# The 60 taps of a convolution, spread over the stages ahead of the attention's second pair

## The chip, the cores and the metric

The kernel runs on one core of a Trainium2 chip. Its engines each follow an instruction queue of their own: TensorE (PE in the profile; its weight loads are PEld), VectorE (DVE), ScalarE (ACT), GpSimd (POOL) and SyncE (SP, which here only issues DMAs). The metric is the time of one execution on the device in microseconds (us).

## What is computed

One layer of a hybrid decoder trunk, 1024 positions of 1024 features, all in float32: an input projection feeds three groups of heads, whose outputs go through one output projection; a gated MLP with a short causal convolution follows.

```
h = rmsnorm(x, ln1_g)
p = h @ w_in
qa, ka, va, log_f        # 6 heads: forgetting attention
qb, kb, vb               # 6 heads: dilated sliding windows
yc = p[..., GV] * sigmoid(p[..., GG])          # 256 channels
yc = causal_dwconv(yc, conv_w, conv_b)         # 31 taps per channel
yc = silu(layernorm(yc, cnorm_g, cnorm_b))
y = concatenate([rmsnorm(ya), rmsnorm(yb), yc])
x = x + y @ w_o
u = causal_dwconv(rmsnorm(x, ln2_g) @ w_up, ffn_conv_w, ffn_conv_b)   # 3 taps
x = x + (silu(u[..., :F]) * u[..., F:]) @ w_down
out = rmsnorm(x, g_final)
```

## The kernel before

Features lie on the partitions and the 1024 positions along a row, so a tile is 128 x 1024, mostly worked on as two halves of 512. Every float32 operand of a matmul is split into a high and a low part (names with `h` and `l`), and a product takes three matmuls (`mm3`, lines 118 to 120). ScalarE copies the high part, GpSimd or VectorE subtracts it to get the low one. Weights come by DMA on SP's queue into two raw buffers (`raw_...`) and are split into `wh_...` (ScalarE) and `wl_...` (GpSimd, line 105), three buffers each.

The part around the change runs in this order. The first gates (`gv0`, `gg0`) are projected while x is loaded. ScalarE takes the sigmoid of `gg` and VectorE multiplies (`gate_mul`, line 259): the product of channel group 0 is `gv` again, `us[0]`. Eight blocks of v (`vps`, lines 278 to 280) follow, each of 24 matmuls into one of two PSUM buffers of tag `mm`. ScalarE copies each out to `vf` (two buffers, line 282) and casts it to three tiles `VS` (line 285); GpSimd adds the forget gates' bias (`fg`, line 287) and takes the low parts (line 286). A block's `vf` is free when GpSimd is done with it. Then come the second gates (`g`, line 254 evicts them), the small logarithm of the forget gates on VectorE (`lf_...`, lines 489 to 501), the first q and k (`qps`, `kps`; VectorE evicts them at lines 298 and 314, ScalarE and GpSimd split them into `QH`, `QL`, `KH`, `KL`), and the attention of six pairs of heads. The gates, q and k use the same two buffers `mm`.

The attention of a pair (`attention`) takes 8 blocks of scores (`s`, lines 376 and 381). VectorE adds the bias and finds the minimum (`w` and `mn`, line 386), ScalarE takes the exponential (line 392), TensorE transposes it (`pt`, line 422), ScalarE and VectorE split that (`ph`, `pl`, lines 426 and 427), and TensorE multiplies by v (`av`, lines 437 and 438); line 467 adds it to `y`. Between these steps `mix` lays the projections of the next pair as fillers (`fills`): pair 0's attention carries the q and k of pair 1, pair 1's those of pair 2 and, from `yc`, the layernorm of the convolution (`conv_norm`). Pair 0's generator also starts pair 1's (`ahead`).

The convolution is `conv_taps(c)`, once for each of the two groups of 128 channels: one first tap (line 531, which makes `yc` from `us`) and 30 more (line 533), each of which reads `us` with a shift and adds into `yc`. The calls stand behind pair 0:

```
            if pr == 0:
                for c in range(2):
                    conv_taps(c)
```

Within an engine the queue's order is fixed when the program is built: a scheduler takes the instructions in the order of the code as priorities and places each where it can start, by its own estimate of times; on the chip each engine runs its queue strictly in that order.

Of the kernel before, what the change touches and what calls it, by code (L numbers as in the profile page):

```python
# [12 lines left out]
ALU = mybir.AluOpType  # L13
# [3 lines left out]
S = 1024  # L17
# [37 lines left out]
C_CB, C_CNG, C_CNB, C_CW = 30, 32, 34, 36  # L55
# [7 lines left out]
def hybrid_trunk(ctx: ExitStack, tc: tile.TileContext, xT, par, win, wvf, wo, wup, wdn,  # L63
# [19 lines left out]
    def col(c):  # L83
        return prm[:, c:c + 1]
# [43 lines left out]
    def drain(gen):  # L128
        for _ in gen:
            pass  # L130

    def mm_all(ps, ws, xs, sl):
        drain(mm_gen(ps, ws, xs, sl))
# [18 lines left out]
    with ExitStack() as cb_:  # L152
# [35 lines left out]
        xs = []  # L188
# [59 lines left out]
        def gates1():  # L248
            for dst, wi in ((us[1], 13), (gsg[1], 15)):
                w = load_chunk(win[wi], 8, f"w{wi}")  # L250
                for i in range(2):
                    ps = mm_ps(f"g{wi}_{i}")
                    mm_all(ps, w, xs, HS[i])
                    V.tensor_mul(dst[:, HS[i]], ps, r1b[:, HS[i]])

        def gate_mul(c):
            A.activation(gsg[c], gsg[c], AF.Sigmoid)
            ln_exp_set()
            V.tensor_mul(us[c], us[c], gsg[c])


        wv = []
# [7 lines left out]
            wv += [(hi[:, j, :], lo[:, j, :]) for j in range(2)]  # L270
        fg = bp.tile([P, NT, NFOX], F32, name="fg")
        VS = [bp.tile([P, NT, 4, 64], F32R, tag="VS", name=f"VS{p}", bufs=3) for p in range(NPAIR)]
        for t in range(NT):
            ps = mm_ps(f"vps{t}")
            sl = slice(P * t, P * t + P)
            for k in range(DT):
                (wh, wl), (xh, xl) = wv[k], xs[k]
                T.matmul(ps[:, 0:390], lhsT=xh[:, sl], rhs=wh, start=k == 0, stop=False)
                T.matmul(ps[:, 0:390], lhsT=xh[:, sl], rhs=wl, start=False, stop=False)
                T.matmul(ps[:, 0:390], lhsT=xl[:, sl], rhs=wh, start=False, stop=k == DT - 1)  # L280
            vf = bp.tile([P, 390], F32, tag="ev", name=f"vf{t}", bufs=2)
            A.activation(vf, ps[:, 0:390], AF.Identity, scale=r1c[:, t:t + 1])
            for p in range(NPAIR):
                src = vf[:, P * p:P * p + P].rearrange("p (h d) -> p h d", d=64)
                A.copy(VS[p][:, t, 0::3, :], src)
                G.tensor_sub(VS[p][:, t, 1:3, :], src, VS[p][:, t, 0::3, :].bitcast(F32))
            G.tensor_add(fg[:, t, :], vf[:, 384:390], prm[:, C_BF:C_BF + NFOX])


        def proj_q(pr, out):  # L290
            QH, QL = pair_tile(f"QH{pr}"), pair_tile(f"QL{pr}")
            out["Q"] = (QH, QL)
            w = load_chunk(win[pr if pr < 3 else pr + 3], 8, f"wq{pr}")
            for i in range(2):
                ps = mm_ps(f"qps{pr}_{i}")
                yield from mm_gen(ps, w, xs, HS[i])
                qs = bp.tile([P, HALF], F32, tag="ev", name=f"qs{pr}_{i}", bufs=2)
                V.scalar_tensor_tensor(qs, ps, -0.125, r1b[:, HS[i]], op0=ALU.mult, op1=ALU.mult)
                h = HS[i]
                A.copy(QH[:, h], qs)  # L300
                G.tensor_sub(QL[:, h], qs, QH[:, h].bitcast(F32))
# [170 lines left out]
        def mix(main, fill, units):  # L472

            due = 0.0
            for weight in main:
                due += weight * units / TOTAL
                while due >= 1:
                    due -= 1
                    next(fill, None)
# [46 lines left out]
            return t  # L526


        def conv_taps(c):
            wc, u, y = C_CW + 31 * c, us[c], yc[c]  # L530
            V.tensor_scalar(y, u, col(wc + 30), col(C_CB + c), op0=ALU.mult, op1=ALU.add)
            for d in range(1, 31):
                V.scalar_tensor_tensor(y[:, d:], u[:, 0:S - d], col(wc + 30 - d), y[:, d:],  # L533
                                       op0=ALU.mult, op1=ALU.add)

        def conv_norm(i):

            q, both = [], []
# [77 lines left out]

        rdd = [[dram.tile([8, P], F32, name=f"rdd{pr}_{f}") for f in range(2)] for pr in range(6)]
        ycd = [dram.tile([P, S], F32, name=f"ycd{c}") for c in range(2)]
        gate_mul(0)
        gates1()  # L620
        gate_mul(1)
        st = {}

        def after(gen, acts):
# [36 lines left out]
            for e in range(3):  # L661
                yield from out1(e)

        drain(proj_q(0, at[0]))
        st["cd"] = decay_sums()
        at[0]["V"] = VS[0]
        drain(proj_k(0, at[0]))
        def start(pr):

            fox = pr < 3  # L670
# [19 lines left out]
        fills = [proj(1, at[1]), fill1(), proj(3, at[3]), fill3(), proj(5, at[5]), last_fill()]  # L690
        mains = {0: start(0)}
        for pr in range(6):
            mix(mains[pr], fills[pr], (30, 32, 49, 48, 48, 30)[pr])
            drain(fills[pr])
            if pr == 0:
                for c in range(2):
                    conv_taps(c)
            if pr == 1:
                for c in range(2):
                    nc.sync.dma_start(ycd[c], yc[c])  # L700
            if pr == 4:
                for c in range(2):
                    t = sp_tile(f"ycr{c}")
                    nc.sync.dma_start(t, ycd[c])
                    split(6 + c, t)
                for c in range(3):
                    split(c, yf[c], C_GFOX + c)
# [644 lines left out]
```

## Time and profile before

| | |
|---|---|
| median of 3 runs | 1369.99 us (1369.96 to 1376.69) |
| the profiled execution | 1368.36 us, span 1366.6 us |
| busy in that span: PE / PEld | 1224.1 us (90%) / 984.6 us (72%) |
| DVE / ACT / POOL | 1022.5 (75%) / 619.6 (45%) / 534.2 us (39%) |
| mean granted clock of TensorE | 0.951 of full speed |
| the 60 taps (line 533) on DVE | 72.4 us, 1282 ns each in the mean |

The span runs from the first to the last instruction of the profiled execution. "Busy" is the time in which an engine has an instruction in work; instructions of one engine overlap a little, so a row of several can be shorter than the sum of their durations. A clock of 1.00 is 2.4 GHz, 0.50 is 1.2 GHz. In brackets at the end of a timeline's row stands how long the engine had been idle and whom it waited for.

### The profile page before, as it was taken

To read this page: it belongs to the slowest core of one execution; us is meant where nothing else is said; L and a number is where in the kernel's file an instruction comes from. 1 tells how busy PE (TensorE), PEld (TensorE's weight loads), DVE (VectorE), ACT (ScalarE), POOL (GpSimd) and SP (SyncE) were. 2 spreads that over 40 slices of the span, in tenths; PEclk is the share of its full clock that TensorE was granted. 3 is DMA by queue.
4 is the path that set the end of the run, shared out by engine and by line. 5 is a ranking of instruction groups with operands and counts; after the bars stand their busy time and mean duration, and the time that the engine had idled before them with its cause. 6 is when DMAs were issued, how large, how long until landed. Compare 5 with 4: busy or idle time off the path is not lost.

```text
span 1366.6 us, 17153 instructions
## 1 busy us (share of the span) xinstructions
PE 1224.1 (90%) x6013; PEld 984.6 (72%) x6013; DVE 1022.5 (75%) x1511; ACT 619.6 (45%) x1134; POOL 534.2 (39%) x397
## 2 busy tenths in 40 slices
PE   7999960699999999999777999999999989999996
PEld 5887750467867786778456888888888867787796
DVE  8422699866546556668999888888888798878776
ACT  6423510357554546533434455454554563534333
POOL 4323149522124212145764111111111366767754
PEclk9999985699999999999989999999999999999998
DMA  6002100011100022232013222332333364535213
GB/s 232 16 31 63 58 20 0 24 46 64 47 30 25 32 68 75 90 95 66 16 31 108 76 103 100 108 116 97 111 108 108 111 190 148 182 97 164 62 35 124
DMA packets 61014, 111.99 MB, mean 82 GB/s; under 512 B 6384, under 2 KB 29696, under 8 KB 60928
## 3 DMA queue, kind: packets, MB, share of 16 engines
q1 hardware_dynamic: 60352, 110.62, 24.7%
q8 instruction: 47, 0.77, 0.2%
q14 instruction: 39, 0.32, 0.1%
q10 hardware_dynamic: 576, 0.28, 0.1%
HBM read 86.94 MB, written 23.93 MB: 81 GB/s over the span
## 4 chain that ended last, share of the span: by engine, by line
PE 43%; DVE 10%; DMA 2%; issue 2%; POOL 2%; ACT 1%; DVEq 0%; POOLq 0%; ACTq 0%
PE mA L118 5%; PE mA L120 5%; PE mA L119 5%; PE m L120 4%; PE m L118 4%; PE m L119 4%; PE d L120 3%; PE d L119 3%; PE d L118 3%; DMA tr<-td 2%; PE dl L120 1%; PE dl L119 1%; PE dl L118 1%; POOL wld L860 1%; DVE hc L1178 1%
## 5 line engine op out<-in xcount | busy, mean ns | idle before, releaser
L860 POOL TENSOR_TENSOR wl<-a,wh 128x512 fp32r<-128x512 f32 x48 | 69.3, 1446 | 295.2 <-ACT wh L859 292.0
L392 ACT ACTIVATE w<-w,mn 128x128 f32<-128x128 f32 (+7 forms) x96 | 73.9, 771 | 102.9 <-DVE mn L386 102.2
L427 DVE TENSOR_TENSOR pl<-pt,ph 128x512 fp32r<-128x512 f32 (+1 forms) x120 | 73.8, 634 | 61.4 <-ACT ph L426 61.2
L422 PE MATMUL pt<-idf,w 128*128 128x128 f32 x432 | 67.9, 277 | 57.8 <-DVE mn L386 57.5
L120 PE MATMUL d<-hc,wld 128*128 128x512 f32 x252 | 101.6, 403 | 8.8 <-POOL wld L860 8.6
L119 PE MATMUL d<-hc,whd 128*128 128x512 f32 x252 | 100.4, 399 | 5.5 <-DVE hc L1178 5.5
L105 POOL TENSOR_TENSOR wl_wk<-raw_wk,wh_wk 128x512 fp32r<-128x512 f32 x12 | 72.1, 6006 | 73.5 <-ACT wh_wk L104 71.1
L118 PE MATMUL d<-hc,whd 128*128 128x512 f32 x252 | 100.2, 398 | 0.2 <-ACT whd L859 0.2
L422 PEld LDWEIGHTS pt<-idf,w 128*128 128x128 f32 x432 | 51.2, 141 | 67.5 <-issue 56.8
L119 PE MATMUL m<-t,wh 128*128 128x512 f32 x208 | 82.9, 399 | 7.5 <-DVE t L773 7.5
L118 PE MATMUL m<-t,wh 128*128 128x512 f32 x208 | 82.3, 396 | 4.9 <-ACT t L772 4.2
L120 PE MATMUL m<-t,wl 128*128 128x512 f32 x208 | 82.5, 397 | 1.3 <-POOL wl L860 1.3
L426 ACT CAST ph<-pt 128x512 fp32r<-128x512 f32 (+1 forms) x120 | 62.1, 540 | 38.0 <-PE pt L422 26.8
L437 PE MATMUL av<-ph,VS 128*128 128x256 f32 x240 | 65.9, 293 | 11.7 <-ACT ph L426 11.3
L533 DVE SCALAR_TENSOR_TENSOR yc<-gv,prm,yc 128x1023 f32<-128x1023 f32 (+29 forms) x60 | 72.4, 1282 | 0.0
L859 ACT CAST wh<-a 128x512 fp32r<-128x512 f32 x84 | 52.0, 621 | 40.6 <-issue 24.3
L860 POOL TENSOR_TENSOR wld<-a_d,whd 128x384 fp32r<-128x384 f32 x48 | 57.9, 1210 | 23.8 <-ACT whd L859 20.6
L120 PEld LDWEIGHTS d<-hc,wld 128*128 128x128 f32 x252 | 48.4, 192 | 24.1 <-POOL wld L860 14.4
L438 PE MATMUL av<-pl,VS 128*128 128x256 f32 x240 | 63.6, 302 | 1.6 <-DVE pl L427 1.6
L437 PEld LDWEIGHTS av<-ph,VS 128*128 128x128 f32 x240 | 46.2, 193 | 23.4 <-ACT ph L426 19.7
L118 PE MATMUL mA<-t,wh 128*128 128x512 f32 x144 | 57.1, 397 | 6.4 <-ACT u L1066 6.4
L119 PEld LDWEIGHTS d<-hc,whd 128*128 128x128 f32 x252 | 48.2, 191 | 17.1 <-DVE hc L1178 7.0
(450 smaller groups left out, 3910.6 us busy)
## 6 DMA issues: line engine op xcount, KB each, us to landing
a<-in_wup SPq DMA_DIRECT2D x88, 256.0 KB, 2.6
tr<-td SPq DMA_DIRECT2D x27, 512.0 KB, 3.6
a_d<-in_wdn SPq DMA_DIRECT2D x48, 192.0 KB, 2.4
td<-cv SPq DMA_DIRECT2D x9, 512.0 KB
td<-ta SPq DMA_DIRECT2D x9, 512.0 KB, 3.5
td<-tb SPq DMA_DIRECT2D x9, 512.0 KB, 3.6
x<-in_xT SPq DMA_DIRECT2D x8, 512.0 KB, 3.7
outT<-fo SPq DMA_DIRECT2D x8, 512.0 KB, 2.8
```

Source lines behind the costliest of these rows:

```text
L105: G.tensor_sub(lo[:, 0:kt], raw[:, 0:kt], hi[:, 0:kt].bitcast(F32))
L118: T.matmul(ps, lhsT=wh, rhs=xh[:, sl], start=first, stop=False, **kw)
L119: T.matmul(ps, lhsT=wh, rhs=xl[:, sl], start=False, stop=False, **kw)
L120: T.matmul(ps, lhsT=wl, rhs=xh[:, sl], start=False, stop=last, **kw)
L392: A.activation(w[:, 0:nk], w[:, 0:nk], AF.Exp, scale=-1.0, bias=mn[h], accum_out=den[qi // 4][:, 4 * h + qi % 4:4 * h + qi % 4 + 1])
L422: T.transpose(pt[:, P * b:P * b + P], ws[2 * i + j, h][:, P * kt:P * kt + P], idf)
L426: A.copy(ph[:, 0:w], pt[:, 0:w])
L427: V.tensor_sub(pl[:, 0:w], pt[:, 0:w], ph[:, 0:w].bitcast(F32))
L437: T.matmul(o, lhsT=vt, rhs=phl[0][:, r], start=kt == 0, stop=False)
L438: T.matmul(o, lhsT=vt, rhs=phl[1][:, r], start=False, stop=kt == 2 * i + 1)
L533: V.scalar_tensor_tensor(y[:, d:], u[:, 0:S - d], col(wc + 30 - d), y[:, d:], op0=ALU.mult, op1=ALU.add)
L860: eng.tensor_sub(lo, t, hi.bitcast(F32))
```

## The change

The 60 taps and the two first taps become a generator (`conv_taps` with a `yield` after each), and the places that drive TensorE draw from it. Channel group 0's product is made ahead of the blocks of v (`gate_mul(0)`); two taps are drawn after each block of v, and one after every second step of the second gates (`between`). The rest of group 0 is drained, group 1's product follows, and its taps are drawn after every second step of the first q, the first k and pair 0's attention; what is left is drained behind pair 0.

```diff
                 for i in range(2):
                     ps = mm_ps(f"g{wi}_{i}")
-                    mm_all(ps, w, xs, HS[i])
+                    drain(between(mm_gen(ps, w, xs, HS[i]), taps, 2))
                     V.tensor_mul(dst[:, HS[i]], ps, r1b[:, HS[i]])
...
+        def conv_taps(c):
+            wc, u, y = C_CW + 31 * c, us[c], yc[c]
+            V.tensor_scalar(y, u, col(wc + 30), col(C_CB + c), op0=ALU.mult, op1=ALU.add)
+            yield
+            for d in range(1, 31):
+                V.scalar_tensor_tensor(y[:, d:], u[:, 0:S - d], col(wc + 30 - d), y[:, d:],
+                                       op0=ALU.mult, op1=ALU.add)
+                yield
+
+        def between(gen, taps, every):
+            for n, x in enumerate(gen):
+                if n % every == every - 1:
+                    next(taps, None)
+                yield x
...
+        gate_mul(0)
+        taps = conv_taps(0)
         for t in range(NT):
...
             G.tensor_add(fg[:, t, :], vf[:, 384:390], prm[:, C_BF:C_BF + NFOX])
+            for _ in range(2):
+                next(taps)
...
-        gate_mul(0)
         gates1()
+        drain(taps)
         gate_mul(1)
+        taps = conv_taps(1)
...
-        drain(proj_q(0, at[0]))
+        drain(between(proj_q(0, at[0]), taps, 2))
...
-        drain(proj_k(0, at[0]))
+        drain(between(proj_k(0, at[0]), taps, 2))
...
-            mix(mains[pr], fills[pr], (30, 32, 49, 48, 48, 30)[pr])
+            mix(mains[pr] if pr else between(mains[pr], taps, 2), fills[pr], (30, 32, 49, 48, 48, 30)[pr])
             drain(fills[pr])
             if pr == 0:
-                for c in range(2):
-                    conv_taps(c)
+                drain(taps)
```

The new lines shift the line numbers: in the changed kernel the first tap is line 264, the others line 267, and lines from the v blocks on stand 18 to 20 further down. In the queues it looks like this.

VectorE in the blocks of v, before: the product of group 0 (`gv_324`), and right behind it the forget gates' logarithm.

```order
L259 TENSOR_TENSOR gv_324<-gv_324,gg_326 128x1024
L489 TENSOR_SCALAR lf_a<-fg 128x48
L490 TENSOR_TENSOR lf_a<-lf_a,fg 128x48
L492 TENSOR_SCALAR lf_t<-lf_z 128x48
L500 TENSOR_SCALAR lf_a<-fg 128x48
L493 RECIPROCAL lf_t<-lf_t 128x48
```

The same place now, with `yc_334` the result of channel group 0: the product, the first tap and 18 taps stand ahead of the logarithm, of which the last two are shown here, and the other 12 between its steps and the evictions of the second gates.

```order
L267 SCALAR_TENSOR_TENSOR yc_334<-gv_324,prm,yc_334 128x1007
L267 SCALAR_TENSOR_TENSOR yc_334<-gv_324,prm,yc_334 128x1006
L509 TENSOR_SCALAR lf_a<-fg 128x48
L267 SCALAR_TENSOR_TENSOR yc_334<-gv_324,prm,yc_334 128x1005
L510 TENSOR_TENSOR lf_a<-lf_a,fg 128x48
L267 SCALAR_TENSOR_TENSOR yc_334<-gv_324,prm,yc_334 128x1004
L512 TENSOR_SCALAR lf_t<-lf_z 128x48
L520 TENSOR_SCALAR lf_a<-fg 128x48
```

A run of 18 taps has moved in ahead of the steps that wait for the last `fg`.

VectorE from the first k to the first scores, before: the two evictions of k (`ks`) and then the minima (`mn`) of the first block of scores.

```order
L314 TENSOR_TENSOR ks_0_934<-kps_0_909,r1b 128x512
L314 TENSOR_TENSOR ks_1_963<-kps_1_938,r1b 128x512
L386 ISA w_0_0_974,mn_0_0_0_988<-s_0_0_0_976,cb_968 128x128
L386 ISA mn_0_0_0_988 128x1
L386 ISA w_0_1_975,mn_0_0_1_990<-s_0_0_1_977,cb_970 128x128
```

The same place now, with `yc_335` the result of channel group 1.

```order
L334 TENSOR_TENSOR ks_0_977<-kps_0_948,r1b 128x512
L267 SCALAR_TENSOR_TENSOR yc_335<-gv_325,prm,yc_335 128x1015
L267 SCALAR_TENSOR_TENSOR yc_335<-gv_325,prm,yc_335 128x1014
L267 SCALAR_TENSOR_TENSOR yc_335<-gv_325,prm,yc_335 128x1013
L267 SCALAR_TENSOR_TENSOR yc_335<-gv_325,prm,yc_335 128x1012
L334 TENSOR_TENSOR ks_1_1010<-kps_1_981,r1b 128x512
L267 SCALAR_TENSOR_TENSOR yc_335<-gv_325,prm,yc_335 128x1011
L406 ISA w_0_0_1021,mn_0_0_0_1035<-s_0_0_0_1023,cb_1015 128x128
L406 ISA mn_0_0_0_1035 128x1
L267 SCALAR_TENSOR_TENSOR yc_335<-gv_325,prm,yc_335 128x1010
L406 ISA w_0_1_1022,mn_0_0_1_1037<-s_0_0_1_1024,cb_1017 128x128
```

Six taps of group 1 now stand between the two evictions and the second minimum; 16 more follow in pair 0's attention, the last one behind the eviction of pair 1's first half of k.

VectorE where pair 0's attention ends, before: behind the first minima of pair 1 the two first taps, and from there on the taps of both groups in turn, between which only pair 0's last steps stand.

```order
L386 ISA w_0_1_1605,mn_0_0_1_1620<-s_0_0_1_1607,cb_1600 128x128
L386 ISA mn_0_0_1_1620 128x1
L531 TENSOR_SCALAR yc_334<-gv_324,prm 128x1024
L531 TENSOR_SCALAR yc_335<-gv_325,prm 128x1024
L427 TENSOR_TENSOR pl_3_1_2_1634<-pt_3_1_2_1628,ph_3_1_2_1633 128x512
L427 TENSOR_TENSOR pl_3_1_3_1646<-pt_3_1_3_1641,ph_3_1_3_1645 128x384
L533 SCALAR_TENSOR_TENSOR yc_334<-gv_324,prm,yc_334 128x1023
L467 TENSOR_TENSOR y_967<-av_3_1_1562,yt_3_1_1657 64x256
L533 SCALAR_TENSOR_TENSOR yc_334<-gv_324,prm,yc_334 128x1022
L413 TENSOR_TENSOR y_967<-y_967,rdb_3_1661 128x256
L533 SCALAR_TENSOR_TENSOR yc_334<-gv_324,prm,yc_334 128x1021
L533 SCALAR_TENSOR_TENSOR yc_335<-gv_325,prm,yc_335 128x1023
```

The same place now.

```order
L406 ISA w_0_1_1665,mn_0_0_1_1680<-s_0_0_1_1667,cb_1660 128x128
L406 ISA mn_0_0_1_1680 128x1
L447 TENSOR_TENSOR pl_3_1_2_1694<-pt_3_1_2_1688,ph_3_1_2_1693 128x512
L447 TENSOR_TENSOR pl_3_1_3_1707<-pt_3_1_3_1702,ph_3_1_3_1706 128x384
L406 ISA w_1_0_1727,mn_1_0_0_1741<-s_1_0_0_1729,cb_1658 128x256
L406 ISA mn_1_0_0_1741 128x1
L487 TENSOR_TENSOR y_1014<-av_3_1_1621,yt_3_1_1718 64x256
```

No tap is left there, and pair 1's second block of scores follows at once. TensorE's queue is the same as before up to the first k, and GpSimd's up to the layernorm's first sum; TensorE's fillers within the first two pairs stand otherwise (in the old queue nearly all of the 48 matmuls of pair 2's q came in a row behind pair 1's first scores), and from the last transposes of pair 1 on every engine's queue is again the old one.

## Rows read from the trace of the kernel before

**Rows 1.** The page: TensorE's total, then two rows of 40 equal slices, in tenths.

```profile
PE 1224.1 (90%) x6013; PEld 984.6 (72%) x6013; DVE 1022.5 (75%) x1511; ACT 619.6 (45%) x1134; POOL 534.2 (39%) x397
...
PE   7999960699999999999777999999999989999996
...
PEclk9999985699999999999989999999999999999998
```

**Rows 2.** By stage: length, busy us of PE, PEld, DVE, ACT, POOL; clock; DMA.

```profile
51.50:76.50 25.00, 25.00 (x143) 25.00 (x142) 0.01 (x1) 8.76 (x25) 8.96 (x24) 1.00 0.00 1
76.50:98.40 21.90, 21.90 (x98) 18.18 (x97) 6.06 (x20) 3.40 (x8) 5.37 (x7) 1.00 0.09 25
98.40:122.40 24.00, 24.00 (x116) 19.81 (x116) 4.48 (x7) 8.20 (x11) 8.97 (x7) 1.00 0.29 89
122.40:176.00 53.60, 51.42 (x340) 39.21 (x341) 30.97 (x83) 30.21 (x68) 10.31 (x8) 1.00 0.18 55
176.00:181.00 5.00, 3.81 (x35) 3.02 (x33) 5.00 (x10) 2.33 (x8) 2.97 (x2) 1.00 0.17 54
181.00:195.70 14.70, 14.68 (x65) 11.06 (x64) 14.45 (x14) 1.15 (x3) 2.19 (x1) 0.88 0.00 0
195.70:250.90 55.20, 0.00 (x1) 0.03 (x1) 55.17 (x50) 0.57 (x2) 55.20 (x1) 0.53 0.00 0
250.90:264.00 13.10, 12.27 (x35) 8.03 (x36) 9.13 (x19) 6.74 (x18) 6.53 (x5) 0.51 0.12 41
264.00:320.00 56.00, 52.88 (x319) 37.97 (x318) 38.69 (x91) 34.25 (x66) 13.95 (x11) 1.00 0.15 49
```

**Rows 3.** TensorE's waits from 40 to 420 us: total us, times, longest us.

```profile
PE pt L422 <- DVE mn L386: 56.9, 3, 55.2
...
PE r1cps L235 <- DVE r1b L147: 2.8, 1, 2.8
```

**Rows 4.** Timeline of VectorE at the taps: start us, us, instruction, count.

```profile
176.74 2.93 DVE L531 TENSOR_SCALAR yc<-gv,prm 128x1024 f32<-128x1024 f32 x2
...
184.13 66.15 DVE L533 SCALAR_TENSOR_TENSOR yc<-gv,prm,yc 128x1021 f32<-128x1021 f32 x56
```

**Rows 5.** Timeline of TensorE ahead of the wait and behind it.

```profile
186.20 0.40 PE L119 MATMUL qps<-xl,wh_wq 128*128 128x512 f32 x1
...
258.91 0.63 PE L119 MATMUL kps<-xl,wh_wk 128*128 128x512 f32 x1
```

**Rows 6.** Timeline of GpSimd in the blocks of v and at the taps.

```profile
53.53 1.30 POOL L286 TENSOR_TENSOR VS<-vf,VS 128x128 fp32r<-128x128 f32 x3 [1.41 <-ACT VS L285]
...
193.51 57.90 POOL L105 TENSOR_TENSOR wl_wk<-raw_wk,wh_wk 128x512 fp32r<-128x512 f32 x1 [14.40 <-ACT wh_wk L104]
```

**Rows 7.** Timeline of VectorE and GpSimd in the gated MLP.

```profile
1077.12 1.28 DVE L968 SCALAR_TENSOR_TENSOR cg<-urg,prm,cg 128x1023 f32<-128x1023 f32 x1
...
1085.40 1.29 POOL L860 TENSOR_TENSOR wl<-s,wh 128x512 fp32r<-128x512 f32 x1 [0.66 <-ACT wh L859]
...
1088.14 3.50 DVE L968 SCALAR_TENSOR_TENSOR cv<-urv,prm,cv 128x1023 f32<-128x1023 f32 x2
1088.39 2.17 POOL L860 TENSOR_TENSOR wl<-s,wh 128x512 fp32r<-128x512 f32 x1 [1.71 <-ACT wh L859]
```

**Rows 8.** Timeline of VectorE in the forget gates' logarithm.

```profile
77.81 0.19 DVE L489 TENSOR_SCALAR lf_a<-fg 128x48 f32<-128x48 f32 x1 [26.30 <-POOL fg L287]
...
80.02 0.21 DVE L495 TENSOR_TENSOR lf_t<-lf_z 128x48 f32<-128x48 f32 x1
80.26 0.19 DVE L496 TENSOR_SCALAR lf_p<-lf_t 128x48 f32<-128x48 f32 x1
```

**Rows 9.** VectorE's waits from 122 to 176 us: total us, times, longest us.

```profile
DVE pl L427 <- ACT ph L426: 9.2, 12, 1.6
DVE y L467 <- ACT yt L466: 6.6, 7, 1.6
```

**Rows 10.** A short stretch at the start, by the columns of the stages above.

```profile
42.00:48.60 6.60, 5.72 (x21) 5.14 (x22) 4.65 (x7) 1.99 (x5) 1.37 (x4) 0.50 0.01 5
```

More of the change, by code (lines that the diff above doesn't have):

```diff
@@ L526, in decay @@
             return t
[L529 to L534, printed above, removed]
         def conv_norm(i):
```

## The prediction

> **What bounds the kernel now.** I read the page first, then busy times by stage, then who waited for whom, then the timelines of VectorE and GpSimd around the worst stretch. TensorE is busy for 90% of the span, so a change pays where TensorE stands still or runs slowly. The reader should see TensorE's one zero, in the seventh of 40 slices, and the clock of 5 tenths in it [rows 1]. The stages say the same: from 51.5 to 176 us TensorE is busy practically without a break at full clock; from 195.7 to 250.9 it does nothing while VectorE and GpSimd are busy throughout; from 250.9 to 264 it works at half clock [rows 2]. The 55.2 us are one wait, that of the transposes of pair 1's first block for the minimum `mn` of its scores [rows 3]. VectorE owes that minimum, but works through the convolution before it: two first taps from 176.74, and from 184.13 a run of 56 taps in 66.15 us, 1.18 us each [rows 4]. So the taps are the path there, and nothing else is.
>
> **What is removed.** The run of taps at that place. TensorE gets back 55.2 us of idle time. At half clock a 128x512 matmul takes 0.63 us against 0.40 [rows 5]; the 12.27 us of work from 250.9 to 264 would take half as long, 6.1 us. From 176 to 181 1.2 us are idle, and the clock of 0.88 from 181 to 195.7 is 3.5 us at half, 1.8 us of work [rows 2]. In all 55.2 + 6.1 + 1.2 + 1.8 = 64.3 us. The projection of pair 2's q that ran from 186 on during the wait was useful work; it moves into pair 1's attention, where it fills gaps (52.88 of 56 us busy, [rows 2]). That could give back up to 3.1 us more; I count nothing.
>
> **What is added.** No operation: 62 VectorE instructions (2 first taps, 60 others) and one earlier sigmoid with its two table loads, the same as before, in front of or behind the same v block. All 62 now stand between 51.5 and the end of pair 0's attention (176), in a fixed row. TensorE is the bound there and VectorE nearly idle at first; the cover is VectorE's free time. I add up VectorE's time over these 124.5 us.
>
> - Its present work: 0.01 + 6.06 + 4.48 + 30.97 = 41.5 us [rows 2].
> - The taps: 1.18 us in the old run, where the two channels take turns [rows 4]. Now one channel's taps follow each other, and each needs the result of the one before. Two small dependent steps start 0.24 us apart and last 0.21 [rows 8], so a step waits for the end of the last and 0.03 more; a lone tap of the gated MLP takes 1.28 [rows 7], which makes 1.31. With other work between them the chain is broken; I take 1.25. 62 x 1.25 = 77.5 us, bounds 73.2 and 81.2.
> - GpSimd. Where both engines read two operands from SBUF they exclude each other: two dependent taps of the gated MLP took 3.50 us with a GpSimd subtraction beside them instead of some 2.5, and that subtraction 2.17 instead of the 1.29 of one alone [rows 7]. GpSimd is busy for 8.96 + 5.37 + 8.97 + 10.31 = 33.6 us in these stages [rows 2], subtracting low parts of v, weights, q and k. VectorE pays for that only where its next instruction is such a one; evictions from PSUM are not. Bounds 0 and 33.6; taps are 77.5 of 119 us of its work, so I take 65%, 22 us.
> - Waits that the fixed row leaves. In pair 0's attention VectorE idles 53.6 - 30.97 = 22.6 us, 15.8 of it for ScalarE's copies `ph` and `yt` [rows 2, 9]. A tap in front of such a wait fills it, one behind it does not; the forget gates (`lf_a`, which waited 26.3 us for GpSimd's last `fg`, [rows 8]) still come only after the last v block. Bounds 0 and 22.6; I take 12, about half.
>
> The sum is 41.5 + 77.5 + 22 + 12 = 153 us against 124.5, 28.5 us more: VectorE takes over as the bound of this stage, and evictions of the gates, of q and k, and the first scores come late. The two PSUM buffers let an eviction be late by one group of matmuls (four groups in 21.90 us, 5.5 each, [rows 2]), so TensorE's first waits appear in the gates. By the low bounds the sum is 114.7 and costs nothing; by the high ones 178.9, 54.4 us.
>
> **The clock.** A wait of 2.8 us at the start (`r1cps`, [rows 3]) is followed by half clock from 42 until 48.6 us [rows 10]: 6.6 us at half, 3.3 lost. In the new stage I count it once; where VectorE is the bound, slow matmuls hide behind it. Bounds 0, and many times (fourth rival).
>
> **Queues.** Behind a late eviction on VectorE stand the next tap and the next scores; on SP's queue, the weight loads wait for GpSimd to free the raw buffers, and the small loads of pair 0's denominators stand behind them. I charge nothing for that: a late small load is a later divide on VectorE, within the 12 us. After pair 1's attention every engine's order is what it was.
>
> **Sum.** 64.3 - 28.5 - 3.3 = 32.5 us. The profiled execution took 1368.36 us, so 1335.9; the median of the runs, 1369.99, lies 1.6 higher, and I forecast 1337 for it.
>
> **A rule against a row.** GpSimd's subtraction of a weight tile from 193.51 lasted 57.90 us, to the end of the run of taps; three subtractions of `VS` take 1.30 together when VectorE rests [rows 6]. It got no turn between some 49 taps. Beside the gated MLP's dependent taps it waited for one only [rows 7].
> The Trainium skill, "SBUF — State Buffer", section "Who interferes with whom", says that the pair of ports shared by VectorE and GpSimd is locked for a whole instruction by whoever starts first and the other fully blocks. By that rule GpSimd waits for one tap at a time, as in [rows 7], and the forecast stands; by the row of 57.90 us it would wait for whole runs, and the third rival's time would hold.
>
> **The rivals.**
> 1. *Taking turns, VectorE the bound* (the forecast): 1337, own range 1322 to 1345. Chance 0.50. For it: the sum above, and that dependent taps leave a gap.
> 2. *The cover holds.* GpSimd's turns fall into VectorE's waits and beside evictions, and the taps stand mostly in front of waits: GpSimd 6 and waits 6 us. 41.5 + 77.5 + 6 + 6 = 131, 6.5 us more, no fall of the clock: 1368.4 - 64.3 + 6.5 = 1311. For it: TensorE stayed busy though VectorE worked 38.69 of 56 us [rows 2]. Against it: that is 69%, and here even this sum gives 95% or more. Chance 0.20.
> 3. *GpSimd gets no turn in a run of taps.* After the first product stand a first tap and 18 taps in a row: 19 x 1.18 = 22.4 us, until 73.9. GpSimd can't split v block 1, its buffer isn't free for block 3's copy, and TensorE, with two PSUM buffers, stops ahead of block 5. A block is 24 of the 143 matmuls in 25 us, 4.2 us, so that is at 76.5 - 3 x 4.2 = 63.9. It goes on some 2 us after 73.9 (GpSimd's 1.30 us for `VS` [rows 6] and the rest for `fg` and ScalarE's copy, an estimate), at 76: 12.1 us, and 3.3 of half clock. From there VectorE has 41.5 + 43 x 1.25 + 65% of 24.65 + 12 = 123 us in 99.5, 23.8 more. 64.3 - 15.4 - 23.8 - 3.3 = 21.8, 1347. For it: the 57.90 us [rows 6]. Against it: the two channels took turns there, so that no tap waited for its forerunner; here each does. Chance 0.24.
> 4. *Slower: the clock falls again and again.* Every wait of TensorE for a late eviction in the gates, q, k and attention that is as long as the 2.8 us brings another 6.6 us at half clock. From about 13 such waits beyond the forecast, 13 x 3.3 = 43 us, the kernel is slower: 1380. For it: there are eight evictions and 16 score blocks at which VectorE may be late. Against it: waits so close together that each starts a new fall would need TensorE idle for 36 us more in this stage; from 264 to 320 the clock held at 1.00 with 3.1 us of waits [rows 2]. Chance 0.03.
>
> That the change doesn't do what it says is excluded by the order: the last tap stands ahead of pair 0's last transposes' `pl`. The remaining 0.03 is the ground between the third and the fourth rival, no measurable change.
>
> **The numbers.** Two times of this kernel less than 0.5% (6.8 us) apart can't be told from no change. The likeliest case gives 1337. The lower half of rival 2, a tenth, lies below 1312; the upper part of rival 3, the rest without change and rival 4 lie above 1354, also about a tenth: 1312 to 1354. Cases 1 to 3 are all faster by more than 0.5%: 0.94; unchanged 0.03; slower 0.03.
>
> **What would show it.** Right: no idle stretch of tens of us; pair 1's scores follow pair 0's last values at once; VectorE above 90% busy from the v blocks to the end of pair 0's attention, taps of 1.27 us mixed with ones of 1.7 to 2.5 beside GpSimd; TensorE at 80 to 85% in the gates, q, k and pair 0, waiting for `g`, `qs`, `ks` evictions and `mn`; pair 0's attention ending near 205 us where it was 176. Wrong: a hole ahead of v block 5 with GpSimd's `VS` lasting tens of us (rival 3); TensorE at 95% there (rival 2); long stretches at half clock (rival 4); or a new wait behind pair 1, which I exclude because the order there is unchanged.

## The result and the profile after

The changed kernel takes 1312.62 us (median of 4 runs, 1311.45 to 1316.13) against 1370.83 for the kernel before on the same chips: a ratio of 0.9571, with a 95% interval of 0.9538 to 0.9604. The forecast was 1337 in a range of 1312 to 1354, so the time lies 0.6 us inside its lower end. The profiled execution took 1316.13 us, the longest of the four, with a span of 1314.3.

The page's lines on TensorE's busy time and clock by slices, as in [rows 1]:

```profile
PE 1220.2 (93%) x6013; PEld 982.4 (75%) x6013; DVE 1029.4 (78%) x1511; ACT 620.6 (47%) x1134; POOL 503.3 (38%) x397
PE   6999899999999999998698999999999979999996
PEclk9999799999999999998798999999999989999998
```

The zero in the seventh slice is gone; what is left is a clock of 7 tenths in the fifth. By stages, with the columns of [rows 2] (v, gates, q and k, pair 0, then all of it from the first product to the end of pair 1's second `ks`, and last the start of pair 1):

```profile
52.90:77.30 24.40, 24.40 (x139) 24.40 (x139) 23.79 (x18) 9.03 (x25) 22.32 (x21) 1.00 0.01 1
77.30:105.00 27.70, 25.87 (x113) 20.60 (x112) 26.67 (x36) 5.73 (x11) 13.07 (x12) 1.00 0.12 39
105.00:133.00 28.00, 25.07 (x131) 19.82 (x129) 27.04 (x24) 6.99 (x11) 14.83 (x8) 1.00 0.25 76
133.00:190.00 57.00, 54.52 (x299) 40.54 (x300) 50.26 (x96) 28.30 (x65) 9.98 (x7) 0.88 0.13 39
52.90:191.66 138.76, 131.52 (x693) 106.50 (x693) 128.75 (x174) 50.69 (x111) 60.45 (x47) 0.95 0.13 41
191.66:205.00 13.34, 12.95 (x89) 9.72 (x88) 7.54 (x26) 8.37 (x24) 3.55 (x3) 1.00 0.08 20
```

VectorE, idle in v before, is 97% busy from the product to the first scores, and GpSimd's busy time is 60.45 us where the same work took 33.86. The same stretch of the kernel before, and the one with the taps behind it:

```profile
50.27:176.40 126.13, 123.95 (x702) 103.72 (x701) 43.14 (x112) 50.89 (x111) 33.86 (x47) 1.00 0.15 45
176.40:261.80 85.40, 28.16 (x121) 20.36 (x121) 83.33 (x90) 10.42 (x28) 65.36 (x6) 0.61 0.03 9
```

So the stage became 12.6 us longer (138.76 against 126.13), and TensorE idles for 7.2 us of it (138.76 - 131.52) where it idled for 2.2 (126.13 - 123.95). TensorE's waits from 40 to 300 us (total, times, longest), as [rows 3]:

```profile
PE pt L442 <- ACT w L412: 4.0, 3, 2.6
PE av L457 <- ACT ph L446: 3.7, 6, 1.4
PE r1cps L235 <- DVE r1b L147: 2.4, 1, 2.4
PE rdp L420 <- DVE den L418: 1.5, 3, 1.1
PE qps L118 <- DVE gg L254: 1.3, 1, 1.3
PE ctp L534 <- DVE lf_c L532: 0.8, 1, 0.8
PE g L118 <- DVE gv L254: 0.5, 1, 0.5
```

None is long. The longest in this stage lies at the start of pair 0's attention. VectorE there, and in v (start, us, instruction, count; line 267 is a tap):

```profile
54.17 0.81 DVE L264 TENSOR_SCALAR yc<-gv,prm 128x1024 f32<-128x1024 f32 x1
55.02 25.72 DVE L267 SCALAR_TENSOR_TENSOR yc<-gv,prm,yc 128x1023 f32<-128x1023 f32 x18
81.25 0.43 DVE L509 TENSOR_SCALAR lf_a<-fg 128x48 f32<-128x48 f32 x1 [0.51 <-POOL fg L305]
...
122.97 7.93 DVE L267 SCALAR_TENSOR_TENSOR yc<-gv,prm,yc 128x1015 f32<-128x1015 f32 x4
130.82 0.68 DVE L334 TENSOR_TENSOR ks<-kps,r1b 128x512 f32<-128x512 f32 x1
131.42 1.26 DVE L267 SCALAR_TENSOR_TENSOR yc<-gv,prm,yc 128x1011 f32<-128x1011 f32 x1
132.60 0.28 DVE L406 CUSTOM_DVE_ANT_0 w<-s,cb 128x128 f32<-128x128 f32 x1
```

TensorE had issued pair 0's first scores at 127.06. VectorE was in four taps that took 7.93 us, 2 each in the mean instead of 1.28, with GpSimd's subtractions of `KL` and two weight tiles between them; the second `ks` and one more tap came behind them, and the scores' minimum at 132.60. TensorE's timeline, and the clock behind it (the stages' columns):

```profile
130.49 0.40 PE L120 MATMUL qps<-xh,wl_wq 128*128 128x512 f32 x1
133.47 0.33 PE L442 MATMUL pt<-idf,w 128*128 128x128 f32 x1 [2.59 <-ACT w L412]
...
137.30 0.69 PE L442 MATMUL pt<-idf,w 128*128 128x128 f32 x2 [1.16 <-ACT w L412]
```

```profile
131.00:134.70 3.70, 1.23 (x5) 0.73 (x5) 3.70 (x5) 1.12 (x3) 1.57 (x1) 0.99 0.20 63
134.70:148.30 13.60, 12.24 (x43) 8.24 (x43) 10.03 (x24) 6.13 (x18) 0.00 (x0) 0.50 0.00 0
```

TensorE stood still for 2.59 us, and at 134.7 the granted clock fell to 1.2 GHz for 13.6 us, into which a second wait of 1.16 falls; the 12.24 us of work there would have taken half as long, so 6.1 us are lost. With the 5.1 us of added idle time that is 11.2 of the 12.6 us. Only 2.6 of these come ahead of pair 0's first scores: the waits for `gg`, `lf_c` and `gv` in the list. GpSimd in the blocks of v, against the 1.30 of three subtractions in [rows 6]:

```profile
59.38 1.17 POOL L305 TENSOR_TENSOR fg<-vf,prm 128x6 f32<-128x6 f32 x1
60.51 3.25 POOL L304 TENSOR_TENSOR VS<-vf,VS 128x128 fp32r<-128x128 f32 x3
63.72 1.17 POOL L305 TENSOR_TENSOR fg<-vf,prm 128x6 f32<-128x6 f32 x1
```

A subtraction that took 0.43 us now takes 1.08 with the wait for the running tap. GpSimd gets in after each tap, sometimes with a bias and a subtraction at once, and just keeps pace with a block (4.3 us).

### The profile page after: what moved, and what is told of

It reads as the page before. It is cut to its first block, busy times and chain, and to the rows that moved or that the text cites. A ratio compares the mean times of both kernels' runs of the same rounds, so it can differ in the third digit from the quotient of the medians.

```text
span 1314.3 us, 17149 instructions
## 1 busy us (share of the span) xinstructions
PE 1220.2 (93%) x6013; PEld 982.4 (75%) x6013; DVE 1029.4 (78%) x1511; ACT 620.6 (47%) x1134; POOL 503.3 (38%) x397
## 5 line engine op out<-in xcount | busy, mean ns | idle before, releaser
L267 DVE SCALAR_TENSOR_TENSOR yc<-gv,prm,yc 128x1023 f32<-128x1023 f32 (+29 forms) x60 | 84.8, 1414 | 1.0
L872 ACT CAST wh<-a 128x512 fp32r<-128x512 f32 x84 | 52.2, 623 | 40.5 <-issue 24.3
L873 POOL TENSOR_TENSOR wld<-a_d,whd 128x384 fp32r<-128x384 f32 x48 | 57.4, 1200 | 22.8 <-ACT whd L872 22.6
L442 PEld LDWEIGHTS pt<-idf,w 128*128 128x128 f32 x432 | 51.6, 142 | 15.8 <-ACT w L412 5.5
L981 DVE SCALAR_TENSOR_TENSOR cg<-urg,prm,cg 128x1023 f32<-128x1023 f32 (+1 forms) x44 | 59.3, 1348 | 2.2 <-ACT cg L977 2.2
```

Of the source, the lines that this page charges most:

```text
L442: T.transpose(pt[:, P * b:P * b + P], ws[2 * i + j, h][:, P * kt:P * kt + P], idf)
L873: eng.tensor_sub(lo, t, hi.bitcast(F32))
L981: V.scalar_tensor_tensor(cc[:, d:], ur[:, 0:S - d], col(wc + 2 - d), cc[:, d:], op0=ALU.mult, op1=ALU.add)
```

## The experiments

Three theories. **A**: the taps fit into VectorE's free time, and TensorE pays only where VectorE is late for something that is wanted at once. **B**: VectorE is the bound of the whole stage, as the forecast summed it. **C**: GpSimd is shut out by a row of taps (the forecast's third rival). To compare the traces I use five marks, which are VectorE's own instructions: the first product, the second, the second `ks` of pair 0, of pair 1 and of pair 3 (start times; the profiled execution of each kernel). Each ratio is against runs of the kernel before on the same chip, with medians from 1370.83 to 1373.01. In v and the gates `before` and seq_run have the same code and differ by 1.5 us, so smaller differences between single traces are not read there. Lengths in us:

| kernel | time (median) | ratio to before (95%) | v, gates | q, k | pair 0 | the three | pair 1 to pair 3's k |
|---|---|---|---|---|---|---|---|
| before | 1370.83 | | 51.2 | 21.0 | 53.3 | 125.4 | 198.3 |
| changed | 1312.62 | 0.9571 (0.9538 to 0.9604) | 52.8 | 25.1 | 60.2 | 138.1 | 128.8 |
| c0_spread | 1332.66 | 0.9726 (0.9703 to 0.9748) | 52.8 | 20.5 | 53.3 | 126.6 | 158.5 |
| c1_spread | 1347.29 | 0.9816 (0.9777 to 0.9856) | 51.2 | 25.1 | 57.7 | 134.1 | 161.7 |
| seq_run | 1373.73 | 1.0021 (1.0003 to 1.0038) | 49.7 | 20.9 | 53.3 | 123.9 | 205.7 |
| two_sums | 1312.73 | 0.9573 (0.9548 to 0.9597) | 53.2 | 25.1 | 59.7 | 138.0 | 128.8 |
| no_taps | 1299.44 | 0.9479 (0.9445 to 0.9513) | 51.6 | 21.0 | 53.3 | 125.8 | 127.3 |
| no_pool | 1296.80 | 0.9455 (0.9427 to 0.9482) | 50.0 | 20.7 | 54.9 | 125.6 | 129.4 |
| k_free | 1308.00 | 0.9538 (0.9514 to 0.9561) | 53.3 | 21.5 | 56.3 | 131.1 | 130.7 |
| qk_free | 1309.29 | 0.9542 (0.9517 to 0.9567) | 52.8 | 20.5 | 56.4 | 129.6 | 133.7 |
| v_low | 1311.75 | 0.9547 (0.9522 to 0.9573) | 52.2 | 25.3 | 62.2 | 139.6 | 127.4 |
| v_low_kfree | 1310.42 | 0.9540 (0.9512 to 0.9568) | 52.2 | 21.1 | 59.5 | 132.8 | 132.1 |
| both_alt | 1341.45 | 0.9758 (0.9725 to 0.9792) | 49.7 | 47.3 | 66.8 | 163.8 | 132.9 |
| extra14 | 1328.14 | 0.9663 (0.9620 to 0.9706) | 65.7 | 22.6 | 63.7 | 152.0 | 127.5 |

**One channel alone.** c0_spread:

```diff
-        drain(between(proj_q(0, at[0]), taps, 2))
+        drain(proj_q(0, at[0]))
...
-        drain(between(proj_k(0, at[0]), taps, 2))
+        drain(proj_k(0, at[0]))
...
-            mix(mains[pr] if pr else between(mains[pr], taps, 2), fills[pr], ...)
+            mix(mains[pr], fills[pr], ...)
```

> Only channel 0's taps stand between the blocks of v and in the gates; channel 1's 31 are written behind pair 0's attention as before, where the order puts them one at a time among pair 1's instructions. Theory A (VectorE's free time takes the taps; TensorE pays only where VectorE is late for something it needs at once): v and the gates cost about 2 us, q, k and pair 0 nothing, and pair 1's attention, where VectorE has 38.7 of 56 us of its own, gets 31 x 1.2 = 37 us more, 76 against 56, so some 20 us: 1370 - 64 + 2 + 20 = 1328. Rival (half the taps moved, half the gain): 1370 - 32 + 6 = 1344, with an idle stretch of some 30 us of TensorE at the old place.

c1_spread draws no taps in v and the gates (those two calls are undone) and drains channel 0's behind pair 0.

> Only channel 1's taps stand in q, k and pair 0's attention; channel 0's 31 are written behind pair 0. Theory A: q, k and pair 0 cost the 10 us that they cost in the changed kernel (late first scores of pair 0, then half clock), pair 1 some 20: 1370 - 64 + 10 + 20 = 1336, about 8 slower than with channel 0 alone. Rival (half and half): 1344, as with channel 0 alone. If GpSimd's turns on VectorE are what costs in v and the gates, this one is the faster of the two, by the 2 to 5 us of those stages.

c0_spread came near A's 1328, far from 1344. Channel 0's taps in v and the gates cost 1.2 us of the three stages (126.6 against 125.4), less than the spread named above. c1_spread's 1347 is over A's 1336 and near the rival's 1344; its four runs spread from 1338.70 to 1349.51, so it decides little. The rival's way is not seen in its trace: no idle stretch of 30 us is left in either kernel. TensorE's longest waits from 40 to 330 us, of c0_spread and then of c1_spread:

```profile
PE pt L442 <- ACT w L412: 7.6, 2, 7.3
PE rdp L420 <- DVE den L418: 6.1, 4, 3.1
PE cmu L138 <- POOL cs L555: 4.8, 1, 4.8
```

```profile
PE pt L440 <- ACT w L410: 11.3, 3, 7.3
```

The 31 taps that stand one at a time among pair 1's instructions cost 31 us there (158.5 against 127.3 without taps), where I had reckoned 20. (c1_spread's trace is of its fastest run, 1338.70; the 8.6 us up to the median it doesn't show.)

**The old row, one channel after the other.** seq_run, on the kernel before:

```diff
-            V.tensor_scalar(y, u, col(wc + 30), col(C_CB + c), op0=ALU.mult, op1=ALU.add)
+            first = V.tensor_scalar(y, u, col(wc + 30), col(C_CB + c), op0=ALU.mult, op1=ALU.add)
+            if c:
+                tc.keep_in_program_order(first)
```

> The kernel before, with channel 1's first tap ordered behind channel 0's last: all 62 stay at the old place, but each needs the result of the one before; some 24 of channel 0 stand in a row, the rest among pair 1's instructions. Theory A: VectorE has the same work between the same two points, so the time stays within 10 us of 1370 (1360 to 1375). Rival: it was the unbroken row alone that cost, 62 taps among other work cost half: 1340. On GpSimd: if its 57.9 us without a turn came from neighbouring taps being independent, then in this dependent row no subtraction of a weight tile takes over 4 us; if it came from VectorE's being busy without a break, one lasts as long as the row, some 28 us.

1373.73, as A expected: the order of the taps within that place gains nothing, since VectorE's work there is the same. Channel 1's taps, which stand nearly one at a time as in c0_spread, gain nothing by that. GpSimd met the row of 23 taps at its beginning, and was not shut out:

```profile
190.64 32.60 DVE L535 SCALAR_TENSOR_TENSOR yc<-gv,prm,yc 128x1016 f32<-128x1016 f32 x23
```

```profile
193.02 2.27 POOL L105 TENSOR_TENSOR wl_wk<-raw_wk,wh_wk 128x512 fp32r<-128x512 f32 x1
195.24 2.26 POOL L105 TENSOR_TENSOR wl_wq<-raw_wq,wh_wq 128x512 fp32r<-128x512 f32 x1
```

**Neighbours that don't depend on each other.** two_sums, for channel 0:

```diff
+            z = y if c else gsg[c]
             for d in range(1, 31):
-                V.scalar_tensor_tensor(y[:, d:], u[:, 0:S - d], ..., y[:, d:], ...)
+                o = z if d % 2 else y
+                if d == 1 and not c:
+                    V.tensor_scalar(z[:, 1:], u[:, 0:S - 1], col(wc + 29), None, op0=ALU.mult)
+                else:
+                    V.scalar_tensor_tensor(o[:, d:], u[:, 0:S - d], ..., o[:, d:], ...)
...
+            V.tensor_add(y[:, 1:], y[:, 1:], z[:, 1:])
```

> The changed kernel, with channel 0's taps going in turn into two sums (one in the dead gate buffer, added at the end by one more instruction), so that no tap needs the result of the one just before it; rows, places and count stay the same but for that one. If independence is what shuts GpSimd out (third rival of the prediction): the VS subtractions behind the first product last until the row of 20 taps ends near 78 us, TensorE stands still for 10 to 16 us ahead of v block 5, about 1326. Rival (GpSimd gets one turn after each instruction of VectorE, whatever the next one needs): VS stays near 1.08 us each, no hole, 1312 to 1316.

1312.73 and no hole: C falls for this form. Three `VS` of GpSimd take 4.28 us, 1.43 each and not the 1.08 expected; then two taps of the row in v, the first with a `VS` beside it, the second with the small `fg` alone:

```profile
63.08 4.28 POOL L312 TENSOR_TENSOR VS<-vf,VS 128x128 fp32r<-128x128 f32 x3
```

```profile
60.19 1.47 DVE L272 SCALAR_TENSOR_TENSOR gg<-gv,prm,gg 128x1017 f32<-128x1017 f32 x1
62.98 1.26 DVE L272 SCALAR_TENSOR_TENSOR gg<-gv,prm,gg 128x1015 f32<-128x1015 f32 x1
```

A turn of 128x128 stretches a tap from 1.26 to 1.47 us.

**Both channels in turn, from q on.** both_alt:

```diff
-        drain(taps)
         gate_mul(1)
-        taps = conv_taps(1)
+        taps = pairs(taps, conv_taps(1))
```

`pairs` steps both channels at each draw; the draws in v and the gates are taken out, and each channel's first tap is held to its written place.

> The changed kernel with no tap in v and the gates: both channels start behind the second product and go in turn, tap by tap, held to their written places in q, k and pair 0's attention, so that neighbours are of different channels as in the row of 56 of the kernel before. For the time: VectorE has 34 us of its own from q to the end of pair 0, 62 x 1.2 = 74 of taps and some 10 of GpSimd's turns, 118 in the 75 us of that stretch: 43 more than the time without taps, 1300 + 43 = 1343. For GpSimd: if taps of two channels in turn shut it out, its subtractions of QL, KL and weights beside rows of 4 to 8 taps last 5 us or more, to the end of the row; if it always gets the next turn, none lasts over 2.6 us, and the 57.9 us have another cause.

The time was met (1341.45). GpSimd beside a row of seven taps:

```profile
126.03 11.24 DVE L268 SCALAR_TENSOR_TENSOR yc<-gv,prm,yc 128x1016 f32<-128x1016 f32 x7
```

```profile
129.64 2.00 POOL L105 TENSOR_TENSOR wl_wq<-raw_wq,wh_wq 128x512 fp32r<-128x512 f32 x1 [2.60 <-ACT wh_wq L104]
132.68 2.34 POOL L105 TENSOR_TENSOR wl_wk<-raw_wk,wh_wk 128x512 fp32r<-128x512 f32 x1 [1.03 <-ACT wh_wk L104]
```

So between neighbours that don't depend on each other GpSimd got in, too. But one later subtraction, in pair 0, took 3.28, over the 2.6 expected: it got in only when both taps of a row of two were done.

```profile
193.90 2.41 DVE L268 SCALAR_TENSOR_TENSOR yc<-gv,prm,yc 128x1000 f32<-128x1000 f32 x2
```

```profile
194.19 3.28 POOL L105 TENSOR_TENSOR wl_wq<-raw_wq,wh_wq 128x512 fp32r<-128x512 f32 x1 [4.35 <-ACT wh_wq L104]
```

**What the taps still cost, and who makes them cost.** no_taps keeps the two first taps and leaves the 60 others out:

```diff
-            for d in range(1, 31):
+            for d in ():
...
```

> The changed kernel without its 60 taps; the two first taps stay, so the convolution's sum is left out and the output is not the reference's. It prices what the taps still cost where they stand now. By the places of VectorE's evictions the stage from the first product to pair 0's last ks takes 138.1 us against 125.4 before, 12.6 more: theory A (TensorE pays only for the late first scores of pair 0 and the half clock behind them) says 1312.6 - 12.6 = 1300, with TensorE's wait for the first transposes of pair 0 gone and no half clock from 146 to 160. The forecast's ledger (VectorE the bound of the whole stage, 28.5 and 3.3 us) says 1312.6 - 31.8 = 1281.

no_pool keeps all taps and takes GpSimd's work from among them: ScalarE makes plain copies in its place, so the low parts are left out (the same for the weights, `QL` and `KL` of pairs 0 and 1, and for `fg`, whose bias is left out):

```diff
-                G.tensor_sub(VS[p][:, t, 1:3, :], src, VS[p][:, t, 0::3, :].bitcast(F32))
+                A.copy(VS[p][:, t, 1:3, :], src)
...
```

> The changed kernel, with GpSimd's low parts of v, of the weights of the gates, q and k, and of q and k of pairs 0 and 1 replaced by plain copies on ScalarE, and the forget gates' bias left out; the output is not the reference's. The taps keep their places and GpSimd takes no turn among them. Theory A: GpSimd's turns lengthen VectorE's work (the taps by some 10 us, small steps by 5), but TensorE pays only the part that makes the first scores of pair 0 late, the turns in q and k, 8.1 us of VectorE there: 1304 to 1308, taps of 1.16 to 1.28 us, and the wait at pair 0's start under 1 us. Rival 1 (VectorE is the bound throughout): all 15 us come back, 1298. Rival 2 (the turns are hidden): 1312, within 2.

Without taps 1299.44, as A said (1300), and not B's 1281: the taps still cost some 13 us, and nothing more is hidden elsewhere. The wait at pair 0's start and the half clock (134.7 to 148.3 us of the changed kernel) are gone. Without GpSimd but with all taps it is as fast, 1296.80, and the three stages take 125.6 us, as long as without taps (125.8). That is not A's 1304 to 1308 but the 1298 of the rival on record, VectorE as the bound throughout: with GpSimd's work gone from among the taps, they cost nothing. In the list of waits of the changed kernel TensorE waits for GpSimd nowhere, so it is by its turns on VectorE that GpSimd costs time. By its time the run does not tell A from the rival, because without the turns VectorE is also in time for the first scores. The stage in no_pool, its taps by line (busy, mean ns), and its row of taps in v:

```profile
51.00:177.29 126.29, 124.63 (x691) 103.08 (x690) 115.47 (x174) 64.42 (x159) 2.73 (x3) 1.00 0.14 45
```

```profile
L270 DVE SCALAR_TENSOR_TENSOR yc<-gv,prm,yc 128x1023 f32<-128x1023 f32 (+29 forms) x60 | 75.9, 1266 | 1.0
```

```profile
53.11 24.87 DVE L270 SCALAR_TENSOR_TENSOR yc<-gv,prm,yc 128x1023 f32<-128x1023 f32 x19
```

VectorE is busy for 115.47 us instead of 128.75 with the same 174 instructions: the turns cost it 13.3, and without them it has 10.8 us left over. So the taps alone fit, and 13 us more do not.

**The same work elsewhere.** k_free holds channel 1's taps to written places: 8 in q, none in k, 14 in pair 0, the rest in pair 1; with the new `F1` the layernorm of the convolution begins later.

```diff
-F1 = (9, 12, 14, 18, 21, 23, 27, 30)
+F1 = (13, 15, 17, 20, 22, 24, 27, 30)
...
-        drain(between(proj_k(0, at[0]), taps, 2))
+        drain(proj_k(0, at[0]))
...
-            mix(mains[pr] if pr else between(mains[pr], taps, 2), fills[pr], ...)
+            mix(between(mains[pr], taps, 2 - pr) if pr < 2 else mains[pr], fills[pr], ...)
...
```

> The changed kernel with the taps of channel 1 held to their written places: 8 in q, none in k, 14 in pair 0's attention, the last 9 among pair 1's first instructions; the convolution's norm begins four units later. Theory A: VectorE reaches pair 0's first scores in time, TensorE does not wait there and the clock holds, which takes back most of the 11.1 us that channel 1's taps cost: 1303, if pair 1, where VectorE has 38.7 of 56 us, takes 9 x 1.2 = 11 more without a wait. Rival (the cost is VectorE's total, wherever its taps stand): 1312.

qk_free does the same with no `between` in q, and a later `F1` still.

> The same with no tap in q either: 14 in pair 0, 17 in pair 1, the convolution's norm still later. Theory A: q and k cost nothing, pair 0 and pair 1 carry 17 to 20 us each beside 31 and 39 of their own, both under their 53 and 56 us: 1301 to 1304. Against it: channel 1's 31 taps behind pair 0 cost some 30 us of pair 1 in an earlier run, so 17 there may already hold up TensorE, and the later norm its third pair's keys: 1310.

As A says, pair 0's first scores come in time and the clock holds at 1.00 over the whole stage; below it TensorE's longest wait from 115 to 200 us:

```profile
51.37:183.20 131.83, 126.48 (x710) 104.82 (x709) 115.43 (x164) 50.62 (x111) 59.51 (x47) 1.00 0.14 43
```

```profile
PE av L459 <- ACT ph L448: 3.1, 3, 1.3
```

7.0 us come back there in k_free, 8.5 in qk_free, and pairs 1 to 3 take 1.9 and 4.9 of them. The times are not A's 1303 and 1301 to 1304: 1308.00 lies halfway to the rival's 1312, and 1309.29 is the 1310 that was held against qk_free. Both are ahead of the changed kernel by their medians, but all three intervals overlap. The stage here also holds 10 and 18 taps fewer, so the place and the amount of VectorE's work are not told apart by these two runs alone.

v_low puts eight low parts in q and k on VectorE (the line below, the same for `KL`, and four weight tiles); v_low_kfree does so on top of k_free:

```diff
-                G.tensor_sub(QL[:, h], qs, QH[:, h].bitcast(F32))
+                (G if pr else V).tensor_sub(QL[:, h], qs, QH[:, h].bitcast(F32))
...
```

> The changed kernel with the low parts of q and k of pair 0 and of the weights of pair 0's k and pair 1's q (eight subtractions of 128x512 in q and k) on VectorE in place of GpSimd. Theory A (GpSimd's turns make pair 0's first scores late): such a subtraction takes GpSimd 1.29 us alone and stretches a tap beside it from 1.26 to 2.0 or 2.2, so a turn costs VectorE some 0.9 us; doing it itself costs 0.69 with both operands in SBUF. 8 x 0.2 = 2 us less work for VectorE in q and k, so 1309 to 1311. Rival: VectorE must wait for ScalarE's high part of each, which puts those waits on its row: 1315 or more.

> The same edit on top of the kernel with no taps of channel 1 in k (1308.0): q and k have the least VectorE work without GpSimd there, and pair 0's first scores are in time. Theory A: 1305 to 1308. Rival, waits for ScalarE's high parts on VectorE's row: 1310.

1311.75 and 1310.42: no gain that is clear of the noise, the second not A's 1305 to 1308 but its rival's 1310. To subtract a 128x512 tile itself costs VectorE 0.68 us (the first line, of v_low), to let GpSimd do it some 0.9 (a tap beside it takes 2.18 instead of 1.26; the second line, of the changed kernel). The stages are a little longer than without the edit. VectorE's new waits for ScalarE's high parts in q and k are 0.8 us in v_low and 2.1 in v_low_kfree, which takes back part or all of the 2 us that A expected.

```profile
112.60 0.68 DVE L105 TENSOR_TENSOR wl_wq<-raw_wq,wh_wq 128x512 fp32r<-128x512 f32 x1
```

```profile
117.58 2.18 DVE L267 SCALAR_TENSOR_TENSOR yc<-gv,prm,yc 128x1018 f32<-128x1018 f32 x1
```

**More taps.** extra14 draws 14 taps more, which go into a dead buffer (`extra`):

```diff
...
-            mix(mains[pr] if pr else between(mains[pr], taps, 2), fills[pr], ...)
+            mix(mains[pr] if pr else between(between(mains[pr], taps, 2), extra, 2), fills[pr], ...)
```

> The changed kernel with 14 more taps in pair 0's attention, one between every fourth step of it, written to a dead buffer and used by nothing. In the changed kernel VectorE idles for 7.4 of pair 0's 60.2 us. Theory A: the cover there is nearly used up, so of 14 x 1.2 = 17 us some 10 to 17 come out as time, 1322 to 1330. Rival (TensorE still is the bound there and VectorE's lateness hides): 1312 to 1316.

15.5 us more by the medians, 12.6 by the two ratios, so the cover is used up. But not where I put them: the order moved all 14 ahead into v and the gates, where they took 19.6 us of VectorE with GpSimd's turns, and that stretch grew by 12.9. So the cover of pair 0 was not tested. The gates there, with a clock of 0.87 and TensorE idle for 7.5 us:

```profile
77.00:116.83 39.83, 32.38 (x127) 25.93 (x127) 38.32 (x46) 7.64 (x12) 12.93 (x14) 0.87 0.08 27
```

Taken together: B's sum is excluded by no_taps. A has the place right, since some 8.5 of the 12.6 us are lost from pair 0's first scores on and the loss shrinks when VectorE is in time there. Its amounts are not right: it missed c1_spread, no_pool, k_free, qk_free and v_low_kfree, and time that comes back at the first scores is partly spent again in the pairs behind. C is excluded for the rows that were run, with one case of 3.28 us left.

## Why the forecast came out as it did

The direction and the gain held: the idle row went, and what it still costs depends on how full VectorE is. The size was off by 24 us, and 1312.62 lies below the 1322 to 1345 that the forecast gave its own case; that it lies in the whole range, by 0.6 us, is owed to the room left for the second rival. The mechanism of the cost held only in part. VectorE did become nearly full (93% busy), but it did not take over as the bound of the stage: TensorE stayed at 95%, the sign that the forecast had named for the second rival, and paid mostly at one place.

- **The gain** (64.3 forecast). By the spans 1366.6 - 1314.3 = 52.3 us were won net; with the cost of 12.6 and the 2.6 by which the profiled run's first product came late (52.91 against 50.28) the gain was 67.5. The table has 69.5 of it up to pair 3's k (198.3 against 128.8), of which 2.0 is given back later. The 3.2 us over the forecast are of the size of the 3.1 that I named and did not count, pair 2's q as filler in pair 1's gaps; that this is their cause was not tested.
- **The cost** (28.5 and 3.3 forecast) is 12.6 us. **The step that failed is the price of GpSimd's turns**, 22 us as 65% of its busy time: they cost VectorE 13.3. In the row of v a tap takes 1.43 us against 1.31 in no_pool (25.72 us for 18, 24.87 for 19), so turns of some 0.43 us of work cost 0.12 a tap there, and 0.21 between the independent taps of two_sums. Only the 128x512 turns in q and k cost about what was charged, some 0.9 of 1.29 us. The other terms: the 77.5 us of taps are 75.9 + 1.6 in no_pool, but neighbours overlap by some 0.08 us each, so that work and taps fill 115.5 us and not 119; waits of 12, taken as half of a bound without a further reason, were 10.0 (138.76 - 128.75); and the sum was set against 124.5 us where the stretch to these marks is 126.1. Together 8.7 + 3.5 + 2.0 + 1.6 = 15.8 us of the 19.2; the rest is the clock's 3.3, but for rounding. That the corrected terms give 12.6 again shows nothing more: busy and idle time of VectorE always add up to the stage.
- **The clock** fell once, as forecast, for 13.6 us and not 6.6, and the 6.1 us that it cost are part of the 12.6, not on top of them. The forecast counted one such fall, its fourth rival one for each wait as long as the 2.8 us of `r1cps`; in this execution `r1cps` itself waited for 2.4 us, and no fall followed.
- **TensorE** was to be 80 to 85% busy with its first waits in the gates. It is 95% busy (131.52 of 138.76, half clock included); in the gates and at q's start it waits 1.8 us, and most of the cost arises at pair 0's first scores, a place that the sum over the whole stage could not show. VectorE's above 90% was right (93%); pair 0 ended at 191, not 205.
- **The rivals.** The time is that of the second (1311), and so is TensorE's share, but its sum is not: it had a cost of 6.5 us and no fall of the clock. Its cost was 6.1 us too low and its gain 3.2 too low, so its time came out in part by luck. The third is excluded by the `VS` rows: no hole, and no three of them over 4.24 us. The fourth: one fall.

The Trainium skill, "SBUF — State Buffer", section "Who interferes with whom", has the engine that comes second wait for the other's one instruction. The runs with taps in rows agree (1.08 and 1.43 us for a `VS`, 2.0 to 2.34 for a weight tile). The 57.90 us of [rows 6] do not, nor do the 3.28 us behind two taps in both_alt, and both stay unexplained: dependent taps, two sums in turn, and two channels in turn in rows of 6 to 8 all let GpSimd in. A row of some 50 independent taps with a GpSimd instruction in its middle was not tried again.

## What to carry to other kernels

To fill an engine's idle time, add up its own work, the new work, and what a second engine takes from it in turns; here the first two fit (115.5 us in 126.3) and with the turns of 13.3 us they no longer did. Then look for the place where the filled engine is wanted at once, here the first scores behind the evictions of k. Keeping that place free brought the clock back here, but only some 4 us by the medians, which is not clear of the noise. Where an order is made by a program, moving lines may not move instructions: look at what stands where.

## What the runs showed of the hardware

- What a turn costs VectorE depends on GpSimd's tile: a 128x128 subtraction stretches an independent tap from 1.26 to 1.47 us, a 128x512 one to some 2.2. A 128x48 step of 0.20 us takes 1.29 when GpSimd's 128x512 turn falls on it (the steps at 87.40 and 98.75 us of the changed kernel).
- The first tap, one tensor operand, takes 0.81 us for 128x1024 beside no GpSimd subtraction, where every other tap, with two, takes some 1.26. In [rows 4] the two took 2.93 beside GpSimd's `KL`.
- One wait of 2.59 us, at pair 0's first scores, was followed by 13.6 us at 1.2 GHz; in k_free, where no wait there is over 1.3 us, the clock held at 2.4. A wait of about that length is not always followed by a fall: `r1cps` at the start waited for 2.4 us in the changed kernel, and the granted clock stayed at 2.4 GHz (1.00 from 36 to 50 us), where 2.8 us in the kernel before were followed by one [rows 3, 10].
